# The second product of the MLP, too, by Strassen's seven multiplications, with its activation sums passing through DRAM

## The chip, the cores and the metric

The kernel runs on one core of one Trainium2 chip. The time of a run is the device time of one execution in microseconds (us). Of the kernel before there are three runs: 1595.16, 1596.98 and 1604.81 us, median 1596.98. One further execution was profiled.

## The reference

One layer of a transformer trunk on 1024 rows of 1024 columns: a combined input projection, two groups of attention heads, an output projection with a gated residual, and then the part that the change is about:

```python
h = rmsnorm(x, g_mlp[l]) * (1.0 + sc2) + sh2
x = x + ga2 * (jnp.square(jax.nn.relu(h @ w_up[l])) @ w_down[l])
return rmsnorm(x, g_final)
```

`w_up` is 1024 x 4096 and `w_down` 4096 x 1024, all float32. A product to float32 accuracy is made of three matmuls: each operand is split in two fp32r halves, high and low, and high by high, high by low and low by high are added up in PSUM (`mm3`).

## The kernel before, in words

The kernel is one stream per engine. Its order is set by a scheduler when the program is built; a number in `early(kind, ...)` moves a step forward in it. Engines run their own stream in order and wait for each other by semaphores. Up to the MLP nothing is touched by the change.

**First product (up).** It is done by Strassen's method already. The 1024 rows are two halves, the 1024 inner columns two halves, and the 4096 output columns are taken in 16 pairs `p` of 2 x 128. For each pair seven products (`11`, `21`, `t2`, `t1`, `t3`, `t4`, `22`; function `product`, L1195 to L1197) of 12 matmuls of 128 x 512 each make the four output tiles. Four subtractions on DVE (L1180 to L1187) make the weights' sums, and seven splits, high half on ACT (L158), low half on POOL (L159), prepare them. DVE adds from PSUM (`ev_add`, L1206), ACT takes the relu and the square, and ACT's queue writes each of the four 128 x 512 tiles of a pair to DRAM (`ud`, L1203 and L1219).

**Second product (down).** Plain. It goes through eight groups `fg` of four inner tiles of 128. For each inner tile the weights (128 x 1024) are loaded, multiplied by the gate on DVE (L171) and split (ACT L172, POOL L173); the activations (128 x 1024) are read back from `ud` and split (ACT L158, DVE L159). Then for each of 8 x 2 output tiles 12 matmuls run into one of four PSUM banks (`dn`, L177 to L179), and DVE adds the bank to the running sum in SBUF (`x1`, L1351). Behind the last group each row tile is squared and summed (ACT), gets its root (POOL), is scaled (DVE, L1362) and written out.

The gate of the MLP is also made inside the up phase, on DVE (`gate_piece`, `gate_finish`, L1257 to L1268); its rows pass through DRAM.

Of the kernel before, what the change touches and what calls it, by code (L numbers as in the profile page):

```python
# [83 lines left out]
def tile_trunk(ctx: ExitStack, tc: tile.TileContext, x, w_mod, w_in, w_uv, w_out, w_up, w_down,  # L84
# [1046 lines left out]
    with ExitStack() as pctx:  # L1131
# [177 lines left out]
        gate3 = bq.tile([P, D], F32, tag="ot", bufs=OTB, name="gate3")  # L1309
        SY.dma_start(gate3, gated[1].to_broadcast([P, D]))  # L1310
        x1 = {}
        NG = DFF // P // FFG
        WD = ((wp, "wh", WHB), (wp, "wl", WLB), (wp, "wh", WHB), (wp, "wl", WLB),
              (gp, "s", 3), (gp, "s", 3), (gp, "s", 3), (bq, "kl", KL))
        for fg in range(NG):
            uh, ul, wdh, wdl = {}, {}, {}, {}
            for f in range(FFG):
                ft = fg * FFG + f
                if fg % 2:
                    wt_ = ((gp, "t", 12), (gp, "t", 12))  # L1320
                else:
                    wt_ = WD[2 * f:2 * f + 2]
                wdh[f], wdl[f] = load_split([P, D], w_down[ft * P:(ft + 1) * P, :], f"d{ft}", *wt_, None, gate3)
                ur = gp.tile([P, S], F32, tag="wro", bufs=2, name=f"ur{ft}")
                SY.dma_start(ur, ud[ft])
                for hf in (1, 0):
                    cs = slice(hf * 512, hf * 512 + 512)
                    if fg % 2 == 0:
                        uh[f, hf], ul[f, hf] = htile(f"uh{ft}_{hf}"), htile(f"ul{ft}_{hf}")
                    else:  # L1330
                        if hf:
                            t_ = gp.tile([P, S], F32R, tag="t", bufs=12, name=f"uh{ft}")
                            t2_ = bq.tile([P, S], F32R, tag="wt", bufs=WT, name=f"ul{ft}")
                        uh[f, hf], ul[f, hf] = t_[:, cs], t2_[:, cs]
                    split(uh[f, hf], ul[f, hf], ur[:, cs])
            if fg == NG - 1:
# [74 lines left out]
```

## Time and profile before

| | |
|---|---|
| runs, median (lowest to highest) | 1596.98 us (1595.16 to 1604.81) |
| the profiled execution: time, span | 1597.82 us, 1596.1 us |
| busy of the span: PE, DVE, ACT, POOL | 90%, 70%, 48%, 41% |
| first matmul of the up phase | at 910.3 us |
| matmuls of the down phase | 1536, from 1231.1 to 1588.4 us |
| mean granted TensorE clock | 0.939 |

How to read it: the span is the profiler's time from the first to the last instruction, the device time lies 1.7 us above. A share of busy time is a mean over the whole kernel. PE's rows have ends that are modelled, so the distance of two starts, not the duration, tells what a matmul costs in a stream. The two phases that are changed fill the last 43% of the span.

### The profile page before, as it was taken

What the parts mean: (1) busy time and instruction counts of PE and PEld (TensorE: products, weight loads), DVE (VectorE), ACT (ScalarE), POOL (GpSimd) and SP (SyncE); (2) the same over time, 40 slices, a digit from 0 to 9 for tenths busy, and PEclk for the clock granted to TensorE, in tenths of its full rate; (3) what the DMA queues carried; (4) which work ended last, traced back from release to release, by engine and by line L of the source; (5) the groups of instructions that cost most, each with busy time, mean ns of one, the idle gap of its engine ahead of it and who ended that gap; (6) DMA issues with size and microseconds to landing.
All of it is one profiled execution on the core that took longest, in us unless ns stands there. A gap on an engine that the chain in (4) does not pass through costs nothing.

```text
span 1596.1 us, 20085 instructions
## 1 busy us (share of the span) xinstructions
PE 1439.3 (90%) x7056; PEld 1186.3 (74%) x7056; DVE 1117.3 (70%) x1963; ACT 761.3 (48%) x1474; POOL 657.7 (41%) x476
## 2 busy tenths in 40 slices
PE   5979968877798869899989989999999999999998
PEld 3758747666687657788778767788888888888886
DVE  7878999999966894998834487454334757565534
ACT  5676465434446535898733454554454312121102
POOL 3343222433345456585553386454442322222101
PEclk8899978978889988999979989999999999999999
DMA  9531221322111221221222245443335723223102
GB/s 325 150 101 42 64 62 40 84 75 92 45 44 40 57 69 66 93 74 47 74 86 89 88 123 170 132 146 111 120 106 186 262 79 131 80 96 105 64 24 95
DMA packets 122373, 157.18 MB, mean 98 GB/s; under 512 B 9584, under 2 KB 81304, under 8 KB 122272
## 3 DMA queue, kind: packets, MB, share of 16 engines
q1 hardware_dynamic: 112624, 139.08, 27.9%
q10 hardware_dynamic: 9648, 16.81, 2.9%
q8 instruction: 56, 0.92, 0.2%
q14 instruction: 45, 0.37, 0.1%
HBM read 118.62 MB, written 33.05 MB: 95 GB/s over the span
## 4 chain that ended last, share of the span: by engine, by line
PE 57%; DVE 28%; DMA 4%; ACT 4%; issue 4%; POOL 3%; SPq 0%; DVEq 0%; POOLq 0%; ACTq 0%
PE dn L177 7%; PE dn L178 7%; PE dn L179 7%; DVE tk_jk L503 4%; DVE tk_jk L529 4%; DVE m L709 4%; PE upb L1195 3%; PE upb L1197 3%; PE upb L1196 3%; DMA wm<-in_w_mod_dram 2%; PE wo L177 2%; PE wo L178 2%; PE upd L1195 2%; PE upd L1197 2%; PE upd L1196 2%
## 5 line engine op out<-in xcount | busy, mean ns | idle before, releaser
L177 PE MATMUL dn<-whd,uh 128*128 128x512 f32 x512 | 199.1, 390 | 0.5 <-DVE x L1351 0.5
L179 PE MATMUL dn<-whd,ul 128*128 128x512 f32 x512 | 199.2, 389 | 0.0
L178 PE MATMUL dn<-wld,uh 128*128 128x512 f32 x512 | 199.2, 389 | 0.0
L173 POOL TENSOR_TENSOR wld<-wrd,whd 128x1024 fp32r<-128x1024 f32 x32 | 79.9, 2505 | 235.4 <-ACT whd L172 215.9
L711 POOL TENSOR_TENSOR be<-be,m 128x895 f32<-128x895 f32 (+7 forms) x64 | 89.5, 1401 | 171.3 <-DVE m L709 111.7
L1351 DVE TENSOR_TENSOR x<-dn,x 128x512 f32<-128x512 f32 x128 | 86.4, 685 | 93.0 <-PE dn L179 93.0
L709 DVE TENSOR_TENSOR_SCAN m<-m 128x896 f32<-128x896 f32 (+7 forms) x64 | 98.8, 1548 | 28.1 <-ACT m L707 25.8
L177 PEld LDWEIGHTS dn<-whd,uh 128*128 128x128 f32 x512 | 96.1, 188 | 21.1 <-DVE x L1351 1.2
L172 ACT ACTIVATE whd<-wrd 128x1024 fp32r<-128x1024 f32 x32 | 33.8, 1056 | 162.6 <-PE dn L178 81.0
L179 PEld LDWEIGHTS dn<-whd,ul 128*128 128x128 f32 x512 | 96.1, 188 | 20.1
L178 PEld LDWEIGHTS dn<-wld,uh 128*128 128x128 f32 x512 | 96.1, 188 | 19.8
L159 DVE TENSOR_TENSOR ul<-ur,uh 128x512 fp32r<-128x512 f32 x64 | 84.0, 1342 | 22.2 <-ACT uh L158 19.3
L159 POOL TENSOR_TENSOR w<-wrup,w 128x512 fp32r<-128x512 f32 x44 | 61.7, 1408 | 71.8 <-ACT w L158 67.5
L159 POOL TENSOR_TENSOR wt<-wrup,wt 128x512 fp32r<-128x512 f32 x48 | 66.9, 1399 | 44.2 <-ACT wt L158 41.7
L529 DVE TENSOR_SCALAR_CACHE_REDUCE tk_jk<-mk,tlo,above 128x384 bf16<-128x384 uint16 (+4 forms) x80 | 74.7, 934 | 2.0
L644 PE MATMUL avs<-wts,va 128*128 128x256 f32 (+1 forms) x320 | 57.8, 311 | 18.5 <-DVE ota L662 8.8
L503 DVE TENSOR_SCALAR_CACHE_REDUCE tk_jk<-mk,thr 128x384 bf16<-128x384 bf16 (+4 forms) x80 | 69.9, 874 | 1.2
L171 DVE TENSOR_TENSOR wrd<-wrd,gate 128x1024 f32<-128x1024 f32 x32 | 45.3, 1414 | 33.3 <-DMA wrd<-in_w_down_dram 33.3
L644 PEld LDWEIGHTS avs<-wts,va 128*128 128x128 f32 x320 | 49.5, 212 | 24.7 <-DVE wts L632 9.4
L158 ACT ACTIVATE uh<-ur 128x512 fp32r<-128x512 f32 x64 | 37.3, 618 | 60.4 <-PE dn L178 50.1
L821 POOL TENSOR_TENSOR dl<-dl,dst 128x896 f32<-128x896 f32 (+4 forms) x40 | 51.3, 1301 | 34.4 <-DVE dst L817 28.2
L552 ACT ACTIVATE tk_jka<-sc,thr 128x1024 uint8<-128x1024 f32 x32 | 37.0, 1156 | 57.9 <-DVE thr L559 49.2
(399 smaller groups left out, 4524.2 us busy)
## 6 DMA issues: line engine op xcount, KB each, us to landing
wrd<-in_w_down_dram SPq DMA_DIRECT2D x32, 512.0 KB
ur<-ud SPq DMA_DIRECT2D x32, 512.0 KB
wrup<-in_w_up_dram SPq DMA_DIRECT2D x28, 512.0 KB
m2raw<-in_w_mod_dram SPq DMA_DIRECT2D x24, 512.0 KB
ud<-c ACTq DMA_DIRECT2D x48, 256.0 KB
wm<-in_w_mod_dram SPq DMA_DIRECT2D x24, 256.0 KB
x<-in_x_dram SPq DMA_DIRECT2D x8, 512.0 KB
wrdq<-in_w_in_dram SPq DMA_DIRECT2D x8, 512.0 KB
```

What stands on the lines that cost most here:

```text
L159: (lo_eng or V).tensor_tensor(lo, src, hi.bitcast(F32), op=OP.subtract)
L173: (lo_eng or G).tensor_tensor(lo, raw, hi.bitcast(F32), op=OP.subtract)
L177: T.matmul(ps, ah, bh, start=start, stop=False)
L178: T.matmul(ps, ah, bl, start=False, stop=False)
L179: T.matmul(ps, al, bh, start=False, stop=stop)
L503: V.tensor_scalar(jk[:, :widths[b]], src or sc[b], t, 0.5 - TOPK, op0=op, op1=OP.add, accum_out=c)
L529: V.tensor_scalar(jk[:, :widths[b]], mk[b].bitcast(U16), tlo[:, j:j + 1], above[:, j:j + 1], op0=OP.is_ge, op1=OP.add, accum_out=cnt[0][:, ...
L644: T.matmul(dst, vv, rhs, start=kt == 0 and l == 0, stop=half and l == 1)
L709: V.tensor_tensor_scan(m[:, :n][:, ::-1], m[:, :n][:, ::-1], m[:, :n][:, ::-1], 1.0, op0=OP.mult, op1=OP.bypass)
L711: G.tensor_tensor(be[:, :n - 1], be[:, :n - 1], m[:, 1:n], op=OP.mult)
L1195: T.matmul(ps, wh_, ah[a, k], start=start and k == 0, stop=False, **skip)
L1351: V.tensor_tensor(xc, ps, xc, op=OP.add)
```

## The change

The down phase is made by Strassen's method, too. Its operands are the four blocks of a pair's activations (two row halves by two inner tiles) and the four 128 x 512 blocks of the two weight tiles.

- The four sums of activations that the method needs are made **in the up phase**, on DVE, right after the squares. ACT's queue writes seven tiles of a pair, not four, to a new DRAM array `uq`, in 512-byte pieces, so that the seven tiles of 128 rows lie side by side.
- In the down phase a pair's activations come back as four tiles of 128 x 896 (one for each row tile `c` of a half), and each is split in one go: ACT the high half, **POOL** the low half (before: DVE).
- The weights of a pair are multiplied by the gate (four times 128 x 512 on DVE), four sums are made (DVE), and seven operands of 128 x 512 are split (ACT; low half six times POOL, once DVE).
- A group `g` is two pairs. For each `c` of a group seven products of 6 matmuls run, each product continuing in a PSUM bank that an earlier one has left its values in: bank `z` takes `11` then `21`, `b` takes `t2`, `t3`, `t4`, `d` takes `t1`, `22`. DVE reads the bank **after each product** (`keep`, L1405), before the next one may add to it. Seven running sums per `c` are kept; they are joined in the last group.
- The gate's loads use another buffer, and the gate is read back in two halves while the up phase still runs.

```diff
-    ud = [dp.tile([P, S], F32, name=f"ud{f}") for f in range(DFF // P)]
+    uq = [dp.tile([4 * P, 7 * P], F32, name=f"uq{p}") for p in range(DFF // P // 2)]
...
+        def put(p, j, t):
+
+            A.dma_start(uq[p].rearrange("(c q) (o n) -> q c o n", q=P, n=P)[:, :, j, :],
+                        t.rearrange("q (c n) -> q c n", n=P))
...
             ev_add(c21, b_, p1)
-            finish(c21, 2 * p, 0)
+            square(c21)
+
+            s_ = bq.tile([P, 2, 512], F32, tag="ot", bufs=OTB, name=f"s_{p}")
+            V.tensor_tensor(u3, c21, c22, op=OP.add)
+            put(p, 3, u3)
+            V.tensor_tensor(c21, r["a11"], c21, op=OP.subtract)
+            put(p, 5, c21)
+            V.tensor_tensor(s_[:, 0], u3, r["a11"], op=OP.subtract)
+            put(p, 4, s_[:, 0])
             yield
             product(d_, "22", "s4", ops, False)
             ev_add(u2, d_, u2)
-            finish(u2, 2 * p + 1, 1)
+            square(u2)
+            put(p, 1, u2)
+            V.tensor_tensor(s_[:, 1], u2, s_[:, 0], op=OP.subtract)
+            put(p, 6, s_[:, 1])
             yield
...
+        def d_ops(p):
...
+            operand("11", b11, G)
+            V.tensor_tensor(b11, b12, b11, op=OP.subtract)
+            V.tensor_tensor(b12, b22, b12, op=OP.subtract)
+            operand("t1", b11, G)
+            operand("22", b22, G)
+            V.tensor_tensor(b22, b22, b11, op=OP.subtract)
+            operand("t2", b22, G)
+            operand("21", b21, G)
+            V.tensor_tensor(b21, b21, b22, op=OP.subtract)
+            operand("t3", b12, G)
+            operand("t4", b21, V)
+            return ops
+
+        def d_act(p, c):
+
+            raw = gp.tile([P, 7, P], F32, tag="wro", bufs=2, name=f"ur{p}_{c}")
+            SY.dma_start(raw, uq[p][c * P:(c + 1) * P, :].rearrange("q (o n) -> q o n", n=P))
...
+            split(hl[0], hl[1], raw, A, G)
+            return hl
+
+        def d_product(ps, j, w, acts, ops, start):
+            skip = {} if start else {"skip_group_check": True}
+            for u in range(2):
+                (uh, ul), o = acts[u], ops[u][w]
+                T.matmul(ps, uh[:, j, :], o[:, 0], start=start and u == 0, stop=False, **skip)
+                T.matmul(ps, uh[:, j, :], o[:, 1], start=False, stop=False, **skip)
+                T.matmul(ps, ul[:, j, :], o[:, 0], start=False, stop=u == 1, **skip)
...
+        def keep(g, c, n, ps):
...
+            if g == 0 and n not in RES:
+                early("ev", A.activation, acc[c, n], ps, AF.Copy)
+            else:
+                early("ev", lambda: V.tensor_tensor(acc[c, n], ps, acc[c, n], op=OP.add))
...
+        def d_rest(g, c, acts, ops, r):
...
+            d_product(b_, 4, "t2", acts, ops, True)
+            keep(g, c, 2, b_)
...
+            d_product(d_, 3, "t1", acts, ops, True)
+            keep(g, c, 5, d_)
+            d_product(z_, 1, "21", acts, ops, False)
+            keep(g, c, 1, z_)
+            d_product(b_, 5, "t3", acts, ops, False)
+            keep(g, c, 3, b_)
...
+            d_product(d_, 6, "22", acts, ops, False)
+            keep(g, c, 6, d_)
+            yield
+            d_product(b_, 2, "t4", acts, ops, False)
+            keep(g, c, 4, b_)
+            yield
```

The weight operands lie in rings: `t` has 12 buffers for the four operands `22`, `21`, `t3`, `t4` of a pair, `11` and `t2` have three each, `t1` four. So while group 3 (pairs 6 and 7) is multiplied, all of pair 8 can be prepared, but of pair 9 only `t1`; its other operands wait until the last row tile of group 3 has used the old ones.

**POOL, in the down phase before**, prepares one weight tile after the other:

```order
L173 TENSOR_TENSOR wld19_12410<-wrd19_12407,whd19_12409 128x1024
L173 TENSOR_TENSOR wld20_12651<-wrd20_12648,whd20_12650 128x1024
L173 TENSOR_TENSOR wld21_12666<-wrd21_12663,whd21_12665 128x1024
L173 TENSOR_TENSOR wld22_12681<-wrd22_12678,whd22_12680 128x1024
L173 TENSOR_TENSOR wld23_12696<-wrd23_12693,whd23_12695 128x1024
```

**POOL now**, at the turn from group 3 to group 4 (`d11_9` is operand `11` of pair 9, `ul8_0` the low half of pair 8's activations for row tile 0):

```order
L159 TENSOR_TENSOR d11_9_12635<-wrd9_0_12623,d11_9_12635 128x512
L159 TENSOR_TENSOR dt1_9_12640<-wrd9_0_12623,dt1_9_12640 128x512
L159 TENSOR_TENSOR d11_10_12924<-wrd10_0_12916,d11_10_12924 128x512
L159 TENSOR_TENSOR ul8_0_12663<-ur8_0_12660,uh8_0_12662 128x896
L159 TENSOR_TENSOR ul9_0_12669<-ur9_0_12666,uh9_0_12668 128x896
L159 TENSOR_TENSOR d22_9_12643<-wrd9_3_12626,d22_9_12643 128x512
L159 TENSOR_TENSOR d21_9_12650<-wrd9_2_12625,d21_9_12650 128x512
L159 TENSOR_TENSOR dt1_10_12929<-wrd10_0_12916,dt1_10_12929 128x512
L159 TENSOR_TENSOR dt3_9_12654<-wrd9_1_12624,dt3_9_12654 128x512
L159 TENSOR_TENSOR dt2_9_12647<-wrd9_3_12626,dt2_9_12647 128x512
L159 TENSOR_TENSOR ul8_1_12727<-ur8_1_12724,uh8_1_12726 128x896
```

What moved: POOL now has the activations' low halves between the weights' ones, 20 instructions for a group where it had four.

**DVE, in the down phase before**, has adds from PSUM (L1351), the low halves of the activations, and the gate's products:

```order
L1351 TENSOR_TENSOR x1_4_0_11240<-dn2_4_0_11848,x1_4_0_11240 128x512
L171 TENSOR_TENSOR wrd14_12102<-wrd14_12102,gate3_11170 128x1024
L1351 TENSOR_TENSOR x1_4_1_11256<-dn2_4_1_11862,x1_4_1_11256 128x512
L159 TENSOR_TENSOR ul14_12112<-ur14_12109,uh14_12111 128x512 x2
L1351 TENSOR_TENSOR x1_5_0_11272<-dn2_5_0_11876,x1_5_0_11272 128x512
L171 TENSOR_TENSOR wrd15_12117<-wrd15_12117,gate3_11170 128x1024
```

**DVE now**, at the same turn from group 3 to group 4 (`acc0_2<-dnb4_0` is the `keep` of product `t2`, group 4, row tile 0; `wrd9`, `wrd10`, `wrd11` are weight blocks in SBUF):

```order
L1363 TENSOR_TENSOR wrd9_3_12626<-wrd9_3_12626,wrd9_0_12623 128x512
L1366 TENSOR_TENSOR wrd9_2_12625<-wrd9_2_12625,wrd9_3_12626 128x512
L1405 TENSOR_TENSOR acc3_4_11743<-dnb3_3_12672,acc3_4_11743 128x512
L1405 TENSOR_TENSOR acc0_0_11375<-dna4_0_12709,acc0_0_11375 128x512
L1405 TENSOR_TENSOR acc0_5_11405<-dnd4_0_12737,acc0_5_11405 128x512
L1340 TENSOR_TENSOR wrd11_0_12949<-wrd11_0_12949,gate3_0_10933 128x512
L159 TENSOR_TENSOR dt4_9_12657<-wrd9_2_12625,dt4_9_12657 128x512
L1405 TENSOR_TENSOR acc0_1_11414<-dna4_0_12709,acc0_1_11414 128x512
L1340 TENSOR_TENSOR wrd11_1_12950<-wrd11_1_12950,gate3_1_10935 128x512
L1405 TENSOR_TENSOR acc0_6_11431<-dnd4_0_12737,acc0_6_11431 128x512
L1340 TENSOR_TENSOR wrd11_2_12951<-wrd11_2_12951,gate3_0_10933 128x512
L1405 TENSOR_TENSOR acc0_2_11397<-dnb4_0_12736,acc0_2_11397 128x512
```

What moved: between two adds from PSUM there now stand operations whose two inputs both lie in SBUF, 18 of them to 28 adds in a group.

## Rows read from the trace of the kernel before

**Rows 1.** Page, part 1: engine, busy us, share of the span, instructions.

```profile
PE 1439.3 (90%) x7056; PEld 1186.3 (74%) x7056; DVE 1117.3 (70%) x1963; ACT 761.3 (48%) x1474; POOL 657.7 (41%) x476
```

**Rows 2.** Stretches up and down: length, busy per engine, clock, DMA share, GB/s.

```profile
1060.00:1100.00 40.00, 40.00 (x176) 32.86 (x175) 16.43 (x20) 19.78 (x34) 19.77 (x16) 1.00 0.37 119
1360.00:1400.00 40.00, 40.00 (x178) 33.13 (x177) 22.37 (x23) 6.21 (x8) 10.00 (x4) 1.00 0.22 79
```

**Rows 3.** Tile `dn`, a third of the matmuls: ns min/median/max, starts.

```profile
L177 PE MATMUL dn<-whd,uh x512: 389/389/499, 1231.1 to 1587.9; 128*128 128x512 f32 x171
```

**Rows 4.** PE in time: start us, us; 78 matmuls between the starts.

```profile
1570.26 0.39 PE L177 MATMUL dn<-whd,uh 128*128 128x512 f32 x1
...
1587.94 0.39 PE L177 MATMUL dn<-whd,uh 128*128 128x512 f32 x1
```

**Rows 5.** Tiles `dn` and `ul`, DVE: ns min/median/max.

```profile
L1351 DVE TENSOR_TENSOR x<-dn,x x128: 673/684/692, 1250.3 to 1588.8; 128x512 f32<-128x512 f32 x128
L159 DVE TENSOR_TENSOR ul<-ur,uh x64: 674/692/2892, 1217.5 to 1520.0; 128x512 fp32r<-128x512 f32 x64
```

**Rows 6.** POOL and DVE in time: POOL alone, both at once, DVE alone.

```profile
986.43 1.29 POOL L159 TENSOR_TENSOR w<-wrup,w 128x512 fp32r<-128x512 f32 x1
...
955.74 1.74 POOL L159 TENSOR_TENSOR w<-wrup_1b,w 128x512 fp32r<-128x512 f32 x1
957.44 1.74 POOL L159 TENSOR_TENSOR wt<-wrup_1b,wt 128x512 fp32r<-128x512 f32 x1
...
957.95 1.77 DVE L1180 TENSOR_TENSOR wrup_0b<-wrup_1b,wrup_0b 128x512 f32<-128x512 f32 x1
...
1352.51 0.69 DVE L1351 TENSOR_TENSOR x<-dn,x 128x512 f32<-128x512 f32 x1
1353.11 0.68 DVE L159 TENSOR_TENSOR ul<-ur,uh 128x512 fp32r<-128x512 f32 x1
```

**Rows 7.** Groups, DVE, 960 to 1240 us: busy us, mean ns, idle before.

```profile
L1187 DVE TENSOR_TENSOR wrup<-wrup,wrup 128x512 f32<-128x512 f32 x12 | 15.6, 1296 | 1.9 <-POOL w L159 1.6
...
L1180 DVE TENSOR_TENSOR wrup<-wrup,wrup 128x512 f32<-128x512 f32 x12 | 10.5, 873 | 32.2 <-POOL w L159 32.2
```

**Rows 8.** POOL: tile `wld`, ns min/median/max; group of 896 wide.

```profile
L173 POOL TENSOR_TENSOR wld<-wrd,whd x32: 2388/2405/2856, 1203.4 to 1517.1; 128x1024 fp32r<-128x1024 f32 x32
...
L821 POOL TENSOR_TENSOR dl<-dl,dst 128x896 f32<-128x896 f32 x8 | 13.5, 1686 | 22.7 <-DVE dst L817 19.1 <-PE dz L179 3.6
```

**Rows 9.** Queues of SP, ACT, 1060 to 1140 us: packets, MB, share.

```profile
q1 hardware_dynamic: 8974, 4.97, 21.8%
q10 hardware_dynamic: 2448, 4.46, 14.8%
```

**Rows 10.** Tiles `ur`, `wrd`, `ud`: ACT's high halves, and issuing a DMA.

```profile
L158 ACT ACTIVATE uh<-ur x64: 612/616/634, 1216.8 to 1517.5; 128x512 fp32r<-128x512 f32 x64
...
L172 ACT ACTIVATE whd<-wrd x32: 1042/1061/1065, 1196.3 to 1516.0; 128x1024 fp32r<-128x1024 f32 x32
...
L1203 ACTq DMA_DIRECT2D ud<-c x32: 326/327/391, 966.7 to 1252.3; - x32
```

**Rows 11.** A gap of PE early in the up phase, stretches behind.

```profile
942.95 0.79 PE L1197 MATMUL upd<-hs1h,wt 128*128 128x512 f32 x1 [2.10 <-POOL wt L159]
...
946.53 0.63 PE L1196 MATMUL upd<-hs1l,wt 128*128 128x512 f32 x1
946.96 0.63 PE L1197 MATMUL upd<-hs1h,wt 128*128 128x512 f32 x1
...
945.00:950.00 5.00, 2.85 (x8) 1.74 (x7) 5.00 (x4) 1.65 (x3) 5.00 (x5) 0.50 0.00 0
950.00:955.00 5.00, 5.00 (x12) 3.91 (x13) 0.82 (x2) 2.92 (x6) 5.00 (x5) 0.50 0.71 220
```

**Rows 12.** DVE's last rows in time.

```profile
1588.82 0.69 DVE L1351 TENSOR_TENSOR x<-dn,x 128x512 f32<-128x512 f32 x1 [0.77 <-PE dn L179]
1591.47 1.42 DVE L1362 SCALAR_TENSOR_TENSOR y<-x,fst,gfin 128x512 f32<-128x512 f32 x2 [1.97 <-POOL fst L134]
```

More of the change, by code (lines that the diff above doesn't have):

```diff
@@ L1218, in up_first @@
             A.activation(c, c, AF.Square)
-            A.dma_start(ud[2 * p][:, 512:1024], c)
+            put(p, 0, c)
+            r["a11"] = c
             yield
@@ L1306, in tile_trunk @@
             pass
[L1309 to L1336, printed above, removed]
@@ new lines, in join, with d_first @@
+        def join(g, c, n, m):
+            if g == NG - 1:
+                (V if n > 4 else G).tensor_tensor(acc[c, n], acc[c, n], acc[c, m], op=OP.add)
+        def d_first(g, c, acts, ops, r):
+            z_ = r["z"] = pp.tile([P, 512], F32, tag="z", bufs=ZB, name=f"dna{g}_{c}")
+            d_product(z_, 0, "11", acts, ops, True)
+            keep(g, c, 0, z_)
+            join(g, c, 4, 0)
+        def d_rest(g, c, acts, ops, r):
+            odd = (4 * g + c) % 2
+            b_, d_ = bank("tr", f"dnb{g}_{c}"), bank("av" if odd else "tr", f"dnd{g}_{c}")
+            z_ = r["z"]
+            d_product(b_, 4, "t2", acts, ops, True)
+            keep(g, c, 2, b_)
+            join(g, c, 2, 0)
+            join(g, c, 6, 2)
+            d_product(d_, 3, "t1", acts, ops, True)
[4 more added lines that the diff above has]
+            keep(g, c, 3, b_)
+            join(g, c, 3, 0)
+            join(g, c, 5, 3)
+            d_product(d_, 6, "22", acts, ops, False)
[4 more added lines that the diff above has]
+            yield
@@ new lines, in d_out @@
+        def d_out(c):
+            fin = {(o + c, ch): acc[c, n] for n, (o, ch) in RES.items()}
+            for tt in (4 + c, c):
+                st = bq.tile([P, 4], F32, tag="st", bufs=4, name=f"fst{tt}")
+                y = bq.tile([P, D], F32, tag="wkL", bufs=WL, name=f"y{tt}")
+                for ch in range(2):
+                    cs = slice(ch * 512, ch * 512 + 512)
+                    A.activation(y[:, cs], fin[tt, ch], AF.Square, accum_out=st[:, ch:ch + 1])
+                G.tensor_tensor(st[:, 0:1], st[:, 0:1], st[:, 1:2], op=OP.add)
+                rstd(st[:, 2:3], st[:, 0:1], D)
+                for ch in range(2):
+                    cs = slice(ch * 512, ch * 512 + 512)
+                    V.scalar_tensor_tensor(y[:, cs], fin[tt, ch], st[:, 2:3], gfin[:, cs], op0=OP.mult, op1=OP.mult)
+                    SY.dma_start(out[tt * P:(tt + 1) * P, cs], y[:, cs])
@@ L1366, in _onehot @@
+            for c in range(4):
+                acts = [d_act(2 * g + u, c) for u in range(2)]
+                r = {}
+                if prev:
+                    next(prev)
+                d_first(g, c, acts, ops, r)
+                if prev:
+                    next(prev)
+                    if pc[0] == NG - 1:
+                        d_out(pc[1])
+                prev, pc = d_rest(g, c, acts, ops, r), (g, c)
+        for _ in prev:
+            pass
+        d_out(3)
 def _onehot():
```

76 lines of the change are left out of this document (47 added, 29 removed).

## The prediction

> **What bounds the kernel now.** I read the busy shares first, then the two changed phases stretch by stretch, then single instructions. PE has the largest share, 1439 of 1596 us, and POOL the smallest [rows 1]. In the up and in the down phase PE is busy all of the time at a granted clock of 1.00, while DVE has 41% and 56%, ACT 49% and 16%, POOL 49% and 25% [rows 2]. So both phases are set by the number of matmuls, and what the other engines do lies beside it. The down phase's matmuls start between 1231.1 and 1587.9 us [rows 3]; 78 of them take 17.68 us, so one costs 0.2267 us, whatever its modelled duration says [rows 4]. What the change removes is on the path; the question is whether what it adds still lies beside it.
>
> **What it removes.** The down phase has 1536 matmuls of 128 x 512, the changed one 7 products x 6 matmuls x 4 row tiles x 8 groups = 1344. 192 x 0.2267 us = **43.5 us less**, if PE stays busy.
>
> **What it adds in the down phase.** Take one group of two pairs. PE needs 168 x 0.2267 = 38.1 us.
>
> DVE has 28 adds from PSUM and 18 operations with both inputs in SBUF (8 products with the gate, 8 sums, 2 low halves). An add from PSUM takes 0.68 us and was never slower than 0.69; back to back two operations are 0.60 us apart [rows 5, 6]. The other kind takes 0.69 us alone, but up to 2.89 us [rows 5]. The rows side by side show why: POOL's operation of 128 x 512 takes 1.29 us alone, and 1.74 us when a DVE operation of this kind is there; DVE's then takes 1.77 us [rows 6]. They take turns: DVE waits until POOL's operation is through, POOL's next one waits some 0.45 us for DVE. In the up phase, with POOL busy half of the time, DVE's subtractions have means of 0.87 to 1.30 us [rows 7]. In the new down phase POOL is busy far more than half, so I take the middle of 1.30 and 1.77, less the 0.09 us by which operations overlap: 1.45 us. The ends are 0.60 (never a wait) and 1.77. DVE then needs 28 x 0.60 + 18 x 1.45 = **42.9 us** a group, between 27.6 and 48.7.
>
> POOL has 12 low halves of 128 x 512 at 1.29 us [rows 6] and 8 of 128 x 896. For these the 128 x 1024 ones have 2.405 us [rows 8], which by the line through both sizes gives 2.13 us; another operation of that very shape has a mean of 1.69 [rows 8], the lower end. 15.5 + 17.0 us, and 18 turns of DVE at 0.45, make 40.6 us, between 29.0 and 40.6. Before, POOL had 10 us in 40 here [rows 2].
>
> So DVE, at 42.9 us, is the slowest of three engines that all stand close to 40, and PE's 38.1 us no longer cover them. The order says where it shows. At the turn from one group to the next, pair 9's operands can only be made when the last row tile of group 3 has used the old ones. From there to the first use of `ul8_1` PE has 42 matmuls, 9.5 us; POOL has five low halves of 512, one of 896, the first high half ahead of them (0.62 us [rows 10]) and six turns of DVE: 11.9 us. On DVE the 12 rows of the last order excerpt, six of each kind, take 12.3 us, and `t3`, which may not add to its bank before `acc0_2` is read, comes 48 matmuls, 10.9 us, after their beginning; then two more SBUF operations and an add (3.5 us) stand ahead of the read that `t4` needs 2.0 us later. Some 2.4 us for the one and 1.5 to 3 us for the other are late: 4 to 5 us a turn, which agrees with 42.9 - 38.1 = 4.8. There are seven turns between eight groups: **+33.6 us**.
>
> **What hides, and what that rests on.** ACT's high halves need 14 x 0.62 us and 8 of less than 1.06 us a group [rows 10], under 18 of 38 us. Reading 448 KB tiles back adds to DMA that stood at 22% [rows 2]. In the up phase DVE gets four more SBUF operations a pair, at 0.87 to 1.30 us 3.5 to 5.2 us in 19, and it is idle 59% there [rows 2]; POOL loses 1.8 us a pair to them, with half of its time free. ACT issues three more DMAs a pair at 0.33 us [rows 10]. But two of the seven writes stand in ACT's queue until DVE has made a sum, and high halves are queued behind: 0 to 1.5 us a pair. The writes become 3584 packets of 512 bytes a pair beside the weights' 2048. A packet took 31 ns on SP's queue (mean 553 bytes) and 77 ns on ACT's (mean 1822 bytes) [rows 9]; by the first the 16 engines are 57% busy in a pair's 19 us, by the second 111%, and the phase would be 33 us longer. The size is that of the first, so I take no wait there. For the whole up phase I put +2 us, in a range from -5 (the gate's steps leave the stretch in which PE starved, [rows 11]) to +33. Up to the first matmul of the up phase the order of all engines is as before: nothing.
>
> Entry into the down phase: 12 low halves and two of activations, some 20 us of POOL, come on top of the last pair's; +4 us, between 0 and 8. The end: behind the last matmul two row tiles are finished, not one, so another pair of DVE operations of 1.42 us [rows 12]; +2 us, 0 to 5.
>
> **The sum**, against the profiled execution of 1597.8 us (0.8 above the median): -43.5 + 33.6 + 2 + 4 + 2 = -1.9, so **1596 us**: the whole gain is eaten by the engines that feed PE. A measurement of this kernel can tell about 1%, 16 us, from no change. Chance 0.43; with DVE's operation between 1.35 and 1.57 us its own range is 1583 to 1611.
>
> **Rivals.**
>
> *Turns alone decide.* If DVE's waits happen to fall where no bank is waited for, only the sum of POOL's time and DVE's turns counts: 40.6 - 38.1 = 2.5 us a group, -43.5 + 17.5 + 8 = -18: 1580 us. For it: POOL has no idle time to lose, DVE has some. Against: the `keep` reads stand in the same queue as the waiting operations. Chance 0.20, a little over half of it below 1582. The Trainium skill, page "SBUF — State Buffer", section "Who interferes with whom", has this as a rule: a DVE instruction with two SBUF inputs and a GpSimd instruction that reads SBUF exclude each other for their whole length, one with an input from PSUM is not touched. The trace agrees with both halves (692 ns at most against 2892), and taken as the only limit it gives this rival's 1580 us.
>
> *PE stays the bound.* Waits as in the up phase before, where PE had none in spite of them: -43.5 + 2 = 1556 us. For it: DVE without waits needs 27.6 us. Against: POOL's load, 29.0 us at the very least, nearly three times what it was. Chance 0.10.
>
> *Slower: the gaps take PE's clock.* At 942.95 us PE had a gap of 2.10 us behind a low half of POOL; from then on matmuls started 0.43 us apart, and the clock was 0.50, the lower of the two levels, through the stretches to 955 us [rows 11]. The 20 matmuls in these lost 0.2 us each, 4 us. If each of seven turns has one gap of about 2 us or more, that is 28 us on top of the forecast: 1624 us. It decides if the 4.8 us fall in one piece; in three of 1.5 it does not. Against: while PE is slow, DVE and POOL catch up, so that part of it pays for a later wait. Chance 0.20.
>
> *The up phase suffers:* 1 us a pair of ACT waiting for DVE, 1612 us. Chance 0.07.
>
> **How the numbers follow.** Predicted: 1596 us, of the likeliest case. Faster by over 1% (below 1582): 0.10 + 0.12 + 0.06 of the forecast's own spread = 0.28. Slower by over 1% (above 1612): 0.17 + 0.04 + 0.06 = 0.27. Within: 0.45. The range leaves out the case of 1556 and the worst of the clock's and of the up phase's: 1563 to 1627.
>
> **What would show it.** 1344 down matmuls, and about 85 to 90% of PE busy in the stretches of the down phase. DVE's SBUF operations there with a mean near 1.5 us, the adds from PSUM still at 0.69. POOL busy three quarters or more. Gaps of PE ended by DVE `acc` and by POOL `ul` or `dt2`, once in 43 us. Wrong would be: PE busy throughout (then 1556), DVE's mean under 1.2 us (then the turns decide), a clock of 0.5 in many slices, or gaps in the up phase ended by ACT.

## The result and the profile after

| | before | after |
|---|---|---|
| median (lowest to highest), us | 1597.46 (1595.16 to 1604.81) | 1652.13 (1649.96 to 1654.64) |
| the profiled execution, us | 1597.82 | 1654.64 |

The ratio is 1.0335, 95% interval 1.0297 to 1.0372: **55 us slower**, and outside the predicted range (1563 to 1627 us).

The page's first part, after ([rows 1] before): 192 matmuls fewer, as the change says, and less of PE busy; DVE and POOL have gained 8 and 13 points.

```profile
PE 1423.2 (86%) x6864; PEld 1154.7 (70%) x6864; DVE 1290.4 (78%) x2167; ACT 820.2 (50%) x1566; POOL 886.6 (54%) x616
```

Two stretches of the kernel before: length, then busy time and count of PE, weight loads, DVE, ACT, POOL, then clock, DMA share, GB/s.

```profile
900.00:1240.00 340.00, 329.27 (x1414) 265.89 (x1413) 183.97 (x235) 174.67 (x318) 185.67 (x133) 0.98 0.43 137
1240.00:1316.00 76.00, 75.50 (x332) 61.85 (x331) 51.94 (x55) 19.11 (x28) 20.18 (x9) 1.00 0.47 164
```

The same of the kernel after, with the rest of its down phase. At 1316 us a turn from one group to the next begins, at 1594 us the sixth after it.

```profile
900.00:1240.00 340.00, 318.38 (x1359) 255.65 (x1358) 214.13 (x284) 167.73 (x307) 186.61 (x135) 0.97 0.53 154
1240.00:1316.00 76.00, 61.45 (x233) 46.46 (x231) 57.91 (x61) 32.35 (x54) 48.32 (x28) 0.89 0.65 207
1316.00:1594.00 278.00, 249.25 (x1009) 194.87 (x1009) 242.34 (x271) 90.70 (x131) 216.04 (x121) 0.95 0.38 121
1594.00:1660.00 66.00, 39.80 (x153) 30.24 (x152) 47.03 (x55) 16.07 (x38) 40.63 (x43) 0.86 0.26 92
```

With 0.2267 us a matmul [rows 4] this gives the whole account:

| stage | how read | lost, us | forecast |
|---|---|---|---|
| up, to 1240 | 1414 - 1359 = 55 matmuls | 12.5 | 2 |
| entry, 1240 to 1316 | 332 - 233 = 99 matmuls | 22.4 | 4 |
| six groups | 278 / 6 = 46.3, less 38.1, times 6 | 49.4 | 28.8 (six turns at 4.8) |
| last group | last matmul at 1642.7; 48.7 less 153 x 0.2267 | 14.0 | 4.8 (the seventh) |
| tail | 10.1 us behind the last matmul, before 7.7 | 2.4 | 2 |
| matmuls saved | 192 | -43.5 | -43.5 |
| sum | profiled: 56.8 | 57.2 | -1.9 |

**What the turn looks like.** PE in time, one turn; in brackets the idle time before the row and what ended it.

```profile
1408.79 0.49 PE L1386 MATMUL dnb<-dt,uh 128*128 128x512 f32 x1 [0.75 <-ACT dt L158]
1409.63 0.50 PE L1386 MATMUL dna<-d,uh 128*128 128x512 f32 x1 [0.35 <-ACT uh L158]
...
1416.70 0.40 PE L1387 MATMUL dnd<-dt,uh 128*128 128x512 f32 x1
1420.10 0.50 PE L1386 MATMUL dnb<-dt,uh 128*128 128x512 f32 x1 [3.00 <-DVE acc L1405]
```

DVE in the same stretch.

```profile
1412.65 2.60 DVE L159 TENSOR_TENSOR dt<-wrd,dt 128x512 fp32r<-128x512 f32 x1
1415.17 0.68 DVE L1405 TENSOR_TENSOR acc<-dna,acc 128x512 f32<-128x512 f32 x1
1415.77 2.00 DVE L1340 TENSOR_TENSOR wrd<-wrd,gate 128x512 f32<-128x512 f32 x1
1417.69 0.68 DVE L1405 TENSOR_TENSOR acc<-dnd,acc 128x512 f32<-128x512 f32 x1
1418.30 1.15 DVE L1340 TENSOR_TENSOR wrd<-wrd,gate 128x512 f32<-128x512 f32 x1
1419.37 0.68 DVE L1405 TENSOR_TENSOR acc<-dnb,acc 128x512 f32<-128x512 f32 x1
```

PE waits for the last of these rows. Its product was through at about 1416.4 us; but this read of 0.68 us stands in DVE's queue behind gate products of 2.00 and 1.15 us, and they behind a low half of 2.60. The gate products (L1340) are for a pair that PE needs only a group later. PE's wait for such reads, added up over the six groups (us, times, longest):

```profile
PE dnb L1386 <- DVE acc L1405: 20.3, 7, 4.2
```

That is 3.4 us of the 8.2 that a group loses. ACT's high halves take 1.2 us more (7.5 in all; the one at this turn had itself waited for DVE's sum L1363), POOL's low half 0.3 (1.6 in all), and the lower clock behind the gaps 1.6: 48 matmuls of the six groups start 0.43 us apart and not 0.23. Some 1.7 us a group lie in shorter gaps. The seventh turn, at 1594 us, is a test that the kernel makes by itself: no later pair is left, so no gate product stands among the reads and POOL has less to prepare, and the longest gap of PE up to 1618 us is this one:

```profile
1604.93 0.50 PE L1386 MATMUL dna<-d,uh 128*128 128x512 f32 x1 [0.51 <-DVE acc L1405]
```

The 14.0 us of the last group come later, from 1618 us on, in gaps of 2.98, 2.68 and 3.15 us: DVE and POOL there have the joining of the sums and the finished rows, too.

Some of DVE's rows over the six groups (count, busy us, mean ns, idle before), then POOL's longest. The reads take what they took before [rows 5]; the 103 operations with SBUF inputs have a mean of 1.41 us (all their rows together, 144.7 us).

```profile
L1405 DVE TENSOR_TENSOR acc<-dnb,acc 128x512 f32<-128x512 f32 x72 | 49.2, 683 | 13.4 <-PE dnb L1388 13.4
...
L1340 DVE TENSOR_TENSOR wrd<-wrd,gate 128x512 f32<-128x512 f32 x24 | 34.6, 1440 | 0.0
...
L159 DVE TENSOR_TENSOR dt<-wrd,dt 128x512 fp32r<-128x512 f32 x12 | 24.4, 2038 | 0.0
...
L1360 DVE TENSOR_TENSOR wrd<-wrd,wrd 128x512 f32<-128x512 f32 x11 | 14.2, 1293 | 0.2
...
L1359 DVE TENSOR_TENSOR wrd<-wrd,wrd 128x512 f32<-128x512 f32 x6 | 4.2, 692 | 9.4 <-POOL d L159 9.4
```

```profile
L159 POOL TENSOR_TENSOR ul<-ur,uh 128x896 fp32r<-128x896 f32 x48 | 111.1, 2337 | 37.1 <-ACT uh L158 32.1 <-DMA ur<-uq 5.0
```

So DVE was busy 242.34 / 6 = 40.4 us a group and idle 5.9, most of it waiting for PE or for POOL, while at the turn PE waited for it.

### The profile page after: what moved, and what is told of

It is laid out like the page before. It is cut to its first block, busy times and chain, and to the rows that moved or that the text cites. A ratio compares the mean times of both kernels' runs of the same rounds, so it can differ in the third digit from the quotient of the medians.

```text
span 1652.8 us, 20402 instructions
## 1 busy us (share of the span) xinstructions
PE 1423.2 (86%) x6864; PEld 1154.7 (70%) x6864; DVE 1290.4 (78%) x2167; ACT 820.2 (50%) x1566; POOL 886.6 (54%) x616
## 4 chain that ended last, share of the span: by engine, by line
PE 38%; DVE 35%; DMA 7%; POOL 7%; issue 6%; ACT 5%; SPq 0%; ACTq 0%; DVEq 0%; POOLq 0%
DVE tk_jk L503 4%; DVE tk_jk L529 4%; DVE m L709 3%; DVE acc L1405 3%; PE upb L1195 2%; PE upb L1197 2%; PE upb L1196 2%; DMA m3raw<-in_w_mod_dram 2%; DMA wm<-in_w_mod_dram 2%; PE wo L178 2%; PE wo L177 2%; DVE m2acc L402 2%; PE wo L179 2%; PE dnb L1386 2%; POOL ul L159 2%
## 5 line engine op out<-in xcount | busy, mean ns | idle before, releaser
L159 POOL TENSOR_TENSOR ul<-ur,uh 128x896 fp32r<-128x896 f32 x64 | 148.1, 2333 | 50.6 <-ACT uh L158 44.8
L1386 PE MATMUL dnb<-dt,uh 128*128 128x512 f32 x192 | 82.5, 431 | 31.4 <-DVE acc L1405 26.4
L158 ACT ACTIVATE dt<-wrd 128x512 fp32r<-128x512 f32 x64 | 39.6, 626 | 126.8 <-DVE wrd L1363 97.8
L158 ACT ACTIVATE uh<-ur 128x896 fp32r<-128x896 f32 x64 | 58.7, 946 | 76.5 <-PE dnb L1387 52.8
L159 POOL TENSOR_TENSOR dt<-wrd,dt 128x512 fp32r<-128x512 f32 x48 | 73.9, 1552 | 23.7 <-ACT dt L158 22.2
L159 POOL TENSOR_TENSOR d<-wrd,d 128x512 fp32r<-128x512 f32 x48 | 70.8, 1490 | 23.0 <-ACT d L158 22.8
L1387 PE MATMUL dnb<-dt,uh 128*128 128x512 f32 x192 | 80.4, 419 | 2.6 <-POOL dt L159 2.6
L1388 PE MATMUL dnb<-dt,ul 128*128 128x512 f32 x192 | 80.2, 418 | 0.0
L1405 DVE TENSOR_TENSOR acc<-dnb,acc 128x512 f32<-128x512 f32 x88 | 60.1, 683 | 19.1 <-PE dnb L1388 16.3
L1386 PEld LDWEIGHTS dnb<-dt,uh 128*128 128x128 f32 x192 | 38.5, 201 | 48.7 <-DVE acc L1405 32.7
L630 POOL TENSOR_TENSOR wts<-wfs,wts 128x512 fp32r<-128x512 f32 (+1 forms) x32 | 50.3, 1580 | 28.3 <-ACT wfs L629 27.2
L707 ACT ACTIVATE m<-sz 128x384 f32<-128x384 f32 (+4 forms) x96 | 46.4, 504 | 35.9 <-DVE cs L580 11.1
```

What stands on the lines that cost most here:

```text
L158: A.activation(hi, src, AF.Copy)
L159: (lo_eng or V).tensor_tensor(lo, src, hi.bitcast(F32), op=OP.subtract)
L1386: T.matmul(ps, uh[:, j, :], o[:, 0], start=start and u == 0, stop=False, **skip)
L1387: T.matmul(ps, uh[:, j, :], o[:, 1], start=False, stop=False, **skip)
L1388: T.matmul(ps, ul[:, j, :], o[:, 0], start=False, stop=u == 1, **skip)
L1405: early("ev", lambda: V.tensor_tensor(acc[c, n], ps, acc[c, n], op=OP.add))
```

## The experiments

All are edits of the changed kernel; the ratios are to the kernel before, with their intervals. The view that compares them best is one stretch of the down phase, 1320 to 1540 us: the period of a group is 220 us x 168 / matmuls. One row for each kernel, in this order: the changed one, then `e1`, `e4`, `e11`, `e12`, `e13`, `e14`, `e5`, `e6`.

```profile
1320.00:1540.00 220.00, 195.96 (x797) 153.15 (x796) 194.88 (x220) 70.02 (x101) 169.50 (x94) 0.95 0.38 125
```

```profile
1320.00:1540.00 220.00, 206.56 (x880) 163.12 (x879) 158.67 (x197) 77.71 (x112) 181.67 (x103) 1.00 0.41 138
```

```profile
1320.00:1540.00 220.00, 202.32 (x842) 160.73 (x840) 169.61 (x235) 109.95 (x151) 93.51 (x61) 0.97 0.42 134
```

```profile
1320.00:1540.00 220.00, 218.89 (x940) 174.94 (x939) 150.64 (x208) 122.73 (x168) 94.02 (x65) 1.00 0.47 144
```

```profile
1320.00:1540.00 220.00, 198.46 (x821) 154.78 (x820) 162.02 (x195) 75.15 (x108) 167.27 (x90) 0.98 0.39 129
```

```profile
1320.00:1540.00 220.00, 200.64 (x835) 156.30 (x834) 192.63 (x229) 78.78 (x112) 98.13 (x60) 0.98 0.40 132
```

```profile
1320.00:1540.00 220.00, 204.88 (x865) 161.67 (x864) 198.54 (x296) 79.04 (x112) 0.00 (x0) 0.99 0.42 136
```

```profile
1320.00:1540.00 220.00, 188.81 (x763) 145.13 (x763) 180.47 (x210) 67.62 (x95) 164.54 (x87) 0.97 0.35 119
```

```profile
1320.00:1540.00 220.00, 184.23 (x715) 136.78 (x714) 179.81 (x224) 64.25 (x90) 153.03 (x82) 0.95 0.32 109
```

The last column is PE's wait for DVE's reads in the stretch, added up.

| run | time, us | ratio, interval | period | DVE, POOL busy a group | PE waits for reads, us of 220 |
|---|---|---|---|---|---|
| changed | 1652.1 | 1.0335 [1.0297, 1.0372] | 46.4 | 41.1, 35.7 | 17.3 |
| e1 | 1632.0 | 1.0222 [1.0191, 1.0253] | 42.0 | 30.3, 34.7 | 6.5 |
| e4 | 1625.7 | 1.0174 [1.0143, 1.0206] | 43.9 | 33.8, 18.7 | 15.3 |
| e11 | 1603.9 | 1.0032 [1.0017, 1.0047] | 39.3 | 26.9, 16.8 | none listed |
| e12 | 1649.9 | 1.0319 [1.0282, 1.0356] | 45.0 | 33.2, 34.2 | 19.5 |
| e13 | 1637.2 | 1.0230 [1.0204, 1.0255] | 44.3 | 38.8, 19.7 | 11.5 |
| e14 | 1626.6 | 1.0172 [1.0152, 1.0193] | 42.7 | 38.6, 0 | 9.2 |
| e5 | 1660.6 | 1.0393 [1.0365, 1.0420] | 48.4 | 39.7, 36.2 | 20.5 |
| e6 | 1685.2 | 1.0557 [1.0534, 1.0581] | 51.7 | 42.2, 36.0 | 33.3 |

### Relieve DVE, relieve POOL, relieve both

`e1`: the gate at the end.

```diff
-                V.tensor_tensor(b[q], b[q], gate3[q % 2], op=OP.mult)
...
+                    V.tensor_tensor(fin[tt, ch], fin[tt, ch], gate3[ch], op=OP.mult)
+                    V.tensor_tensor(fin[tt, ch], fin[tt, ch], xr[:, cs], op=OP.add)
```

> The gate multiplies the finished sums (two DVE operations for each of 16 output tiles, at the end), not the weights: DVE has 10 operations with two SBUF inputs in a group of the down phase, not 18, and the residual is no longer loaded at the phase's beginning. Theory A, DVE's queue at the turn: PE waits there for reads of a bank that stand behind these operations. The period of 46 us a group falls to 39 to 41, the gaps of 3 us ended by DVE acc are gone, the entry gives back some 5 us, the tail takes 3 us more: about 1600 us (1590 to 1612). Theory B, POOL's own load (32 to 36 us busy of 46) sets the period: POOL only loses 8 turns of DVE at 0.45 us, the period stays above 42, about 1622 us, with PE's gaps ended by POOL ul and dt.

The period is 42.0 us and the clock stays at 1.00. That is between the two theories, and the time, 1632 us, is in neither's range: 20 us now lie behind the last matmul, where DVE has 32 more operations, 10 us more than in the changed kernel; I had put 3 more. A gap remains at each turn, 1.3 us and not 3. DVE and PE in `e1`, the same place of a turn:

```profile
1393.83 0.68 DVE L1400 TENSOR_TENSOR acc<-dnb,acc 128x512 f32<-128x512 f32 x1
1397.26 1.75 DVE L1361 TENSOR_TENSOR wrd<-wrd,wrd 128x512 f32<-128x512 f32 x1 [2.75 <-POOL d L159]
1398.93 0.68 DVE L1400 TENSOR_TENSOR acc<-dnb,acc 128x512 f32<-128x512 f32 x1
...
1399.66 0.50 PE L1384 MATMUL dnb<-dt,uh 128*128 128x512 f32 x1 [1.31 <-DVE acc L1400]
```

DVE is not even busy: the sum at the head of its queue overwrites what POOL still reads, waits 2.75 us for that, and the read for PE stands behind it.

`e4`: POOL freed of the activations.

```diff
-            split(hl[0], hl[1], raw, A, G)
+            A.activation(hl[0], raw, AF.Copy)
+            A.activation(hl[1], raw, AF.Copy)
```

> POOL's low halves of the activations are left out (ACT writes a second copy of the high halves in their place): POOL has 12 operations of 128x512 in a group and nothing else, DVE all its 46, ACT 8 more of about 1.1 us. Theory A, DVE's operations with two SBUF inputs are long because POOL is there: their mean falls from 1.4 us to about 1.0, the gaps of 3 us at the turns go or halve, the period falls from 46 to about 40 us: 1600 to 1615 us. Theory B, DVE is slow by the number of its operations alone: the mean stays at 1.4 and the period above 44, 1640 us or more.

The low halves of the activations are left out here, as in `e11`. The even pairs' gate products take 0.68 us instead of 1.07, those of the odd pairs 0.80 instead of 1.44. But the period is 43.9 us, and the gap of 3 us is still there (2.95 us at 1367.98): theory A was right on the durations and wrong on what they bring; the time is in neither's range.

`e11`: both edits.

> Both reliefs together: the gate at the end (DVE 10 operations with two SBUF inputs a group, not 18) and POOL without the low halves of the activations (left out, ACT copies the high halves instead). Alone they brought the period from 46.2 to 42.3 and to about 43.5 us. Theory A, the turn is long because DVE and POOL have more to do there than PE's matmuls cover, and nothing else: with both relieved PE is the bound, period 38.1 to 39 us, 1597 to 1607 us (the tail keeps the 20 us that the gate at the end costs). Theory B, the turn has a wait of its own (ACT, the ring of operands): the period stays at 41 us or more, 1618 us and up.

As A expected, with the period just above its 39: PE is busy 218.89 of 220 us, the clock is 1.00, the period 39.3 us, and the kernel, with its long tail and its entry, comes within 1.0017 to 1.0047 of the one before. What the turn loses comes from DVE's and POOL's work, and no other wait is hidden behind it. The reliefs add up: 4.4 us a group the one, 2.5 the other, 7.1 both; 1.2 us stay above PE's 38.1. The reliefs hold what the clock gives back: in this stretch 35 matmuls of the changed kernel start 0.43 us apart, as in [rows 11], which is 1.5 us a group, and none do in `e1` and `e11`.

### Give POOL's work to DVE

`e12`: `e1`, two low halves a group from POOL to DVE, and the gate's loads in their old buffer.

```diff
-            operand("21", b21, G)
+            operand("21", b21, V if p % 2 else G)
-            operand("t3", b12, G)
+            operand("t3", b12, V if p % 2 else G)
```

> The gate at the end, the gate's loads in their old buffer, and of each group two low halves of weights (21 and t3 of the odd pair) made by DVE, which has 10 of 42 us idle there, not by POOL, which is busy throughout the turn. Theory A: the up phase gives 8 us, and at the turn POOL's two operations less (some 3 us) shorten the period from 42.3 to 40.5 to 41.5 us: 1632 - 8 - 9 = 1615 us (1608 to 1620). Theory B, DVE's queue at the turn is what is late, whoever works: two more operations there lengthen the period to 43 us or more: 1628 us or more.

B: the period is 45.0 us, though DVE and POOL are each busy 33 to 34 us a group, both less than PE's 38.1. The sums of the engines do not set the period. PE waits 19.5 us for reads in the stretch, in `e1` 6.5, while DVE itself waits 58 us for PE's products. DVE and PE in `e12`, at a turn:

```profile
1390.95 2.46 DVE L1363 TENSOR_TENSOR wrd<-wrd,wrd 128x512 f32<-128x512 f32 x1
1393.34 0.68 DVE L1399 TENSOR_TENSOR acc<-dnb,acc 128x512 f32<-128x512 f32 x1
...
1394.07 0.50 PE L1383 MATMUL dnb<-dt,uh 128*128 128x512 f32 x1 [1.94 <-DVE acc L1399]
```

`e13` and `e14`: `e1`, with the activations' and then all low halves on DVE.

```diff
-            split(hl[0], hl[1], raw, A, G)
+            split(hl[0], hl[1], raw, A, V)
...
-            operand("11", b11, G)
+            operand("11", b11, V)
```

> The gate at the end, and all low halves of the activations on DVE, not on POOL; nothing is left out. DVE gets 8 operations of 128x896 a group (about 1.05 us each, from 0.60 us for 512 columns), 28 x 0.60 + 10 x 1.2 + 8 x 1.05 = 37 us; POOL keeps 12 operations, 16 to 20 us. Theory A, what counts is the sum of the time in which the two exclude each other: POOL's 8 x 2.3 us become 8 x 1.05, the period falls from 42.3 to 39.5 to 41 us, 1612 to 1622 us. Theory B, the place in DVE's queue decides: the reads for PE stand behind 8 more operations of 1 us, the period is 43 us or more, 1636 us and up.

> As the one before, and the low halves of the weights on DVE, too: POOL has nothing in the down phase, so DVE never waits for it: 28 x 0.60 + 22 x 0.60 + 8 x 1.05 = 38.4 us a group, as much as PE's 38.1. Theory A: the exclusion is gone, and DVE's time alone sets the period, 39 to 41 us: 1608 to 1622 us. Theory B, a queue without slack: each operation that is in the way of a read at the turn costs PE, the period is 43 us or more, 1636 us and up.

`e13` goes B's way (44.3 us), `e14` between both (42.7 us, 1627 us). In `e14` no operation waits for POOL any more. Two of DVE's groups in it, 1320 to 1540 us:

```profile
L159 DVE TENSOR_TENSOR ul<-ur,uh 128x896 fp32r<-128x896 f32 x42 | 44.7, 1084 | 0.7 <-ACT uh L158 0.6
...
L1358 DVE TENSOR_TENSOR wrd<-wrd,wrd 128x512 f32<-128x512 f32 x10 | 6.9, 688 | 0.2
```

DVE's sum is 38.6 us, as worked out, and the period is 4 us longer, with DVE idle for those; PE waits 9.2 us of the 220 for reads and 5.9 for ACT's high halves.

### Change the place of the reads

`e5`: banks of their own.

```diff
-            d_product(b_, 5, "t3", acts, ops, False)
-            keep(g, c, 3, b_)
+            own("z", 3, 5, "t3")
```

> The changed kernel with a PSUM bank of its own for every product but 22 (11, 21, t2, t3, t4; t1 and 22 still share one): no product continues in a bank that DVE has yet to read, a bank comes round again only after 9 to 13 us. DVE and POOL do the same work; six sums are joined in the last group, not five. Theory A, PE waits at the turn because a read stands late in DVE's queue: the gaps ended by DVE acc (20 us between 1300 and 1590) go to under 5, the period falls from 46 to the 42 to 43 us that DVE's own operations need: about 1628 us (1618 to 1636). Theory B, PE waits for operands, and the read is only what comes last: other gaps (ACT dt, POOL dt or ul) take their place, the period stays at 45 or more, 1645 us and up.

The time is B's, and of the mechanism each has a part: PE waits 7.1 us of the 220 for POOL's low halves (1.3 in the changed kernel), but still most for reads. The gaps moved: `t1` and `22` now use the one bank `av` for every row tile (before, every second), and PE waits for its reads. PE in `e5`:

```profile
1372.16 0.67 PE L1386 MATMUL dnd<-dt,uh 128*128 128x512 f32 x1 [4.67 <-DVE acc L1405]
```

`t1` and `22` still share a bank, so the run does not tell what more banks would be worth.

`e6`: hold the next pairs' weights back.

```diff
+                        V.tensor_copy(b[q][:, 0:1], acc[1, 1][:, 0:1])
                     SY.dma_start(b[q], w_down[...])
```

> The changed kernel with the weights of the next two pairs held back: each raw tile gets one column from a running sum of row tile 1 before it may be loaded, so that the gate products and sums of the pairs that PE does not need yet come after the turn, and not between the reads of the turn. Same operations, and six copies of 128x1 a group more on DVE. Theory A, the place in DVE's queue: the gap of 3 us goes to 1 or less, the clock does not fall, the period is 42 to 43 us: about 1625 us (1615 to 1635). Theory B, the sum of DVE's time: what is taken out of the turn is missing later, the reads are late there, the period stays at 45 or more: 1645 us and up.

5 us a group worse, a time of theory B's. The gate products did leave the turn, but the load that they need now starts late, and DVE stands at the head of its queue for it. DVE in `e6`, 1316 to 1594 us:

```profile
L1352 DVE TENSOR_TENSOR wrd<-wrd,gate 128x512 f32<-128x512 f32 x20 | 22.1, 1150 | 12.8 <-DMA wrd<-in_w_down_dram 12.8
```

I had moved a wait, not taken one away; the run says nothing on the place alone. `e8` has `e5`, `e6` and `e7` (below) together:

> All three together: own banks, weights held back, the gate's loads a pair earlier. Theory A: the gains of the up phase and of the turn add up, and with both remedies at the turn PE waits for neither; period 41 to 43 us, 1605 to 1620 us. It stays above the 1597 us of the kernel before, as DVE's sum (about 42 us a group) is longer than PE's 38.1 and the entry still loses some 15 us. Theory B (sums of DVE or waits for operands): 1635 us or more.

1719.3 us, ratio 1.0757 [1.0724, 1.0790]: 67 us above the changed kernel, where `e5` and `e6` alone are 8.5 and 33 above it. Why it is more than their sum stays open.

### The up phase

The changed kernel's gaps, PE, and DVE's wait for the gate's loads, 980 to 1110 us:

```profile
994.67 0.51 PE L1195 MATMUL upb<-h22h,wt 128*128 128x512 f32 x1 [2.71 <-DVE u L1209]
1013.61 0.50 PE L1195 MATMUL upb<-h22h,wt 128*128 128x512 f32 x1 [2.95 <-DVE u L1209]
```

```profile
L1275 DVE SCALAR_TENSOR_TENSOR m3acc<-m3raw,c_act,m3acc 128x512 f32<-128x512 f32 x9 | 10.0, 1107 | 14.6 <-DMA m3raw<-in_w_mod_dram 14.5
```

`e2` leaves the sums out, `e3` makes the gate in the down phase (and uses it at the end), `e7` uses each load a pair later, `e9` puts the loads back into their old buffer.

```diff
 e2
-            V.tensor_tensor(u3, c21, c22, op=OP.add)
-            put(p, 3, u3)
+            put(p, 3, c22)
 e3
-                gates[p - 2]()
...
+                if 1 <= g < 6 and c % 2 == 1:
+                    gates[2 * (g - 1) + c // 2]()
 e9
-            raw = bq.tile([P, 2, 512], F32, tag="kl", bufs=KL, name=f"m3raw{c}_{k2}")
+            raw = bq.tile([P, 2, 512], F32, tag="ot", bufs=OTB, name=f"m3raw{c}_{k2}")
```

> Leaves the four sums of activations of each pair out (other tiles are written in their place, so all seven writes stay). After the change the up phase has lost some 60 matmul slots (13 us) to three gaps of PE between 990 and 1040 us. Theory A, the gate's loads: they were moved into the ring of the operand 22 and come late, DVE stands waiting for them and PE behind it. The three gaps stay, with DVE m3acc waiting for DMA m3raw: 1648 to 1655 us. Theory B, the sums load DVE: the gaps go, 1638 to 1642 us.

> As the kernel that multiplies by the gate at the end, and the gate itself is made in the down phase (two steps in each of groups 1 to 5), its loads in a buffer of their own. Theory A (the gate's loads cost the up phase three gaps): no gap of PE between 990 and 1040 us, 10 to 13 us less than the kernel with the gate last; DVE's 16 more operations of a group of five lie beside PE: about 1588 us (1580 to 1597), faster than both kernels. Theory B (the sums cost them): the gaps stay, and the down phase gets 16 operations more: 3 to 8 us above the kernel with the gate last.

> The changed kernel, with each of the gate's loads in the up phase used one pair later than it is issued; the sums stay. Theory A, the gate's loads came late in the ring of the operand 22: no gaps of PE between 990 and 1040 us, 9 to 12 us less: 1641 us (1638 to 1645). Theory B, DVE's sums make the gaps: 1649 us or more.

> The changed kernel with the gate's loads of the up phase back in the buffer that they had before the change; the four sums stay (two of them are now written into tiles that are free anyway). Theory A, the loads came late in the ring of the operand 22: the gaps of PE between 990 and 1040 us go, DVE waits for DMA m3raw less than 10 us (21 us in the changed kernel), 8 to 12 us less: 1642 us (1639 to 1646). Theory B, the sums and their writes make the gaps: 1649 us or more.

The stretch 900 to 1240 us, in this order: `e2`, `e3`, `e9`.

```profile
900.00:1240.00 340.00, 324.04 (x1378) 259.55 (x1377) 169.82 (x231) 169.06 (x310) 187.58 (x138) 0.97 0.56 162
```

```profile
900.00:1240.00 340.00, 327.13 (x1407) 265.03 (x1407) 201.50 (x273) 175.64 (x320) 193.50 (x141) 0.98 0.52 150
```

```profile
900.00:1240.00 340.00, 324.83 (x1381) 260.23 (x1379) 225.31 (x287) 168.60 (x308) 194.25 (x137) 0.97 0.55 158
```

Before there were 1414, after 1359; of the kernels whose edit leaves this phase alone the count reaches 1375 (`e6`). `e3`, with all the sums and no gate in the phase, has 1407: 32 to 48 of the 55 lost come back (7.3 to 10.9 us). That is theory A, but not for A's reason alone: in `e9` DVE waits for the loads 3.7 us (980 to 1110 us) instead of 16, and only 6 to 22 come back, since new gaps stand between 960 and 1000 us, where more of the gate's steps now lie (ratio 1.0357 [1.0326, 1.0389], no gain). `e2` (1.0333 [1.0299, 1.0368], theory A's time) gets 3 to 19; with the sums gone DVE waits for the loads even longer (33 us between 900 and 1240 us, in the changed kernel 20). `e7` (1.0334 [1.0308, 1.0359], theory B's time) did not do what it says: the first four of its eight loads are issued where they were, within 4 us, and DVE waits 19 us for the loads. Shown is that the gate's steps on top of the sums cost the phase; how this divides between late loads and DVE's time is open. And `e3` as a whole is no faster than `e1` (1.0235 [1.0196, 1.0274]; 1634.8 us, near B's time): it has 34 matmuls more than `e1` up to 1240 us, and 46 fewer from there to 1594 us, where the steps now lie.

### The entry

`e10` leaves the residual out.

```diff
-                if n in RES:
-                    SY.dma_start(acc[c, n], x1d[...])
```

> Leaves the residual out: in group 0 all running sums are copied out of PSUM by ACT, and nothing is loaded into them. The entry (1240 to 1300 us) loses some 22 us. Theory A, a good part of it is DVE standing for the loads of the residual at the head of its queue (4.3 us, three times): 6 to 10 us less, 1642 to 1646 us. Theory B, the entry is lost to the preparation of the first operands on POOL and DVE: 1650 us or more.

1649.3 us, 1.0321 [1.0299, 1.0344]: B, a little under its 1650 us. From 1240 to 1316 us it has the 233 matmuls of the changed kernel. What helps is less work: `e1` has 263 there, `e4` 259, `e11` 290 and `e14` 301, of 332 before. The entry is lost to the preparation of the first operands: of the 99 matmuls 30 come back without the gate products, and 38 more with the low halves on DVE. The longest gap is the turn's mechanism again, at the last pair of the up phase. DVE and PE in the changed kernel:

```profile
1249.02 3.42 DVE L1348 TENSOR_TENSOR wrd<-wrd,gate 128x512 f32<-128x512 f32 x2
...
1252.96 0.68 DVE L1209 TENSOR_TENSOR u<-upb,p 128x512 f32<-128x512 f32 x1
...
1253.70 0.80 PE L1195 MATMUL upb<-h22h,wt 128*128 128x512 f32 x1 [5.13 <-DVE u L1209]
```

The read that PE waits for stands behind gate products of the down phase's first pairs. Behind it PE runs at the lower clock for a while: 28 matmuls of the entry start 0.43 us apart, some 5.6 of the 22.4 us.

## Why the prediction was wrong

**The matmuls saved, -43.5:** right; 6864 instead of 7056, at 0.2267 us.

**The turns, +33.6:** the step that failed. Six of them cost 49.4 us, 8.2 each and not 4.8; the seventh cost next to nothing, but the last group lost 14.0 us where its joins and outputs stand in the queues, which I had not priced. The inputs were right: DVE's operations with SBUF inputs 1.41 us (1.45 taken), the reads 0.68, POOL busy 78% (three quarters or more), DVE's work 40.4 us a group (42.9). What failed is the next sentence, that the slowest engine's sum less PE's 38.1 us is what a turn costs. The period is 46.3 us, 5.9 above DVE's work, because the engines wait for each other in turn: PE for DVE's reads at the turn, DVE for PE's products and POOL's operands elsewhere, and what DVE idles there it cannot work ahead. `e1` and `e12` show it plainly: with both engines under 35 us the period is 42 and 45. My second working, along the order (2.4 us for the one wait, 1.5 to 3 for the other), agreed with the sum, and I took this for a proof. By the rows these two waits are 0.3 and 3.4 us, 3.7 together; the other 4.5 of the 8.2 us are ACT's high halves (1.2), the lower clock (1.6, which I had left to a rival) and short gaps, and neither working had them in it. That the two workings gave the same number was luck. That the burst at the turn comes from the ring of operands is read from the order; no run has more buffers, so it is not shown.

**The entry, +4 (0 to 8):** 22.4 us. I counted POOL's 20 us of low halves and let PE's last pair hide most of them. DVE and POOL were there already at work on that pair's sums, and each delayed the other: PE's gap of 5.13 us, for a read of the last up pair behind gate products, was in no term of mine; with both relieved (`e11`) (332 - 290) x 0.2267 = 9.5 us stay lost.

**The up phase, +2 (-5 to +33):** 12.5 us. I costed the sums and the writes, and put the gate's steps down as a gain; on top of the sums they are the cost (`e3`), and whether by their new buffer or by DVE's time is open. The DMA share was as worked out (57%; 56% in the stretch that answers to [rows 2]).

```profile
1060.00:1100.00 40.00, 40.00 (x176) 32.84 (x175) 22.90 (x30) 18.34 (x32) 17.97 (x13) 1.00 0.56 165
```

**The tail, +2:** 2.4 us.

**The rivals.** *The gaps take PE's clock* (0.20) had the right side and part of the mechanism: in five of the six turns the clock falls to the lower level, as in [rows 11]. Two stretches after the change, and a group without such a fall:

```profile
1324.00:1328.00 4.00, 0.33 (x2) 0.00 (x0) 4.00 (x5) 0.00 (x0) 4.00 (x4) 0.80 0.83 263
1328.00:1332.00 4.00, 3.45 (x8) 2.78 (x9) 2.66 (x4) 0.63 (x1) 2.10 (x2) 0.50 0.18 42
1408.79:1453.98 45.19, 39.79 (x169) 31.17 (x169) 41.54 (x47) 15.16 (x23) 36.71 (x21) 1.00 0.38 128
```

But this group, with the clock at 1.00 throughout, takes 45.2 us against a mean of 46.3: by this one group the clock costs about 1 us a turn, by the count of slow matmuls above 1.6, not 4, and 1624 us would still have been short. *Turns alone decide* (1580 us) fell: in `e14` DVE and POOL have no turns to take, and the period is 42.7. The Trainium skill, page "SBUF — State Buffer", section "Who interferes with whom", agrees with the durations here (the same sum of DVE takes 0.69 us with POOL idle, L1358 of `e14`, and 1.29 us after the change, L1360); as the only limit it gave that rival. *The up phase suffers* (0.07) named ACT waiting for DVE; it was PE waiting for DVE.

No experiment beats the kernel before. `e11` comes nearest, and it leaves part of the computation out; of those that compute everything `e14` is the fastest, 1.0172.

## What to carry to other kernels

When three engines all come near the time of a fourth, the longest sum is a lower bound for the period and no estimate: look for the place where work arrives in a burst, and add what the slow engine idles elsewhere. An operation that nobody needs soon still delays whoever waits behind it in an in-order queue, so I would not put the reads that free a bank in one queue with preparation whose length another engine sets; no run here tries them on another engine. A remedy that delays work (a hold, a later use) needs the order and the load behind it looked up first; two of mine moved a wait to the head of the same queue.
